# A two-layer hybrid decoder trunk on one core: inputs arranged in use order, and the triangular inverse with its small matmuls interleaved

## The chip, the cores and the metric

The kernel runs on one core of a Trainium2 chip. The metric is device time in microseconds (us) of one execution; the arrays are arranged on the host before the launch, and that is not part of the time. The time before is the median of three executions.

## What is computed

Two layers of the same form, on x of 256 positions by 2048 channels. One wide projection of the normalised input (7692 columns) feeds three mixers, whose gated outputs go together through one output projection and are added to x:

```python
for l in range(DEPTH):                      # DEPTH = 2, S = 256, D_MODEL = 2048
    h = rms_norm(x, norm_w[l])
    u = h @ w_in[l]                         # 2048 x 7692
    (c_in, c_gate, g_q, g_k, g_v, g_z, g_b, g_a, a_q, a_k, a_v, a_gate) = jnp.split(u, cuts, axis=-1)
    y_conv = conformer_conv(c_in, ...) * silu(c_gate)       # GLU, 31-tap depthwise conv, LayerNorm, 512 x 512
    y_gdn = gated_deltanet(g_q, g_k, g_v, g_z, g_b, g_a, ...)  # delta rule: a unit lower triangle is inverted
    y_att = dilated_attention(a_q, a_k, a_v, cos, sin) * silu(a_gate)
    x = x + jnp.concatenate([y_conv, y_gdn, y_att], axis=-1) @ w_out[l]
return rms_norm(x, final_norm_w)
```

## The kernel before

All work is written as tasks (Python generators) that name an engine, an estimated cost and the instruction. A planner, `Plan.run`, takes at each step the task that can start first by its estimates (then the lower priority number) and emits its instruction, so each engine's instruction stream is fixed when the program is built; on the chip each engine works through its stream in order and waits by semaphores.

TensorE (PE) carries the projections. A matrix product is made in three terms: weights and activations are each split in a rounded part and a remainder (`whi`, `wlo`; `HT[0]`, `HT[1]`), and hi*hi, hi*lo and lo*hi are added in PSUM. The two-row-block weight pieces (chunks: 256 rows by 384, 396 or 512 columns) are loaded by `load_weights` from the SP queue into four `RAW` buffers; ACT makes `whi` (line 182), DVE `wlo` (line 190), in three buffers each; `project` runs the chunks' matmuls (line 453) in a fixed list of jobs. The first job is GZ+384 (396 columns, 9 chunks in layer 0: two of one row block, then seven pairs), the second and third are the two K blocks of the delta rule, and so on; the convolution's pointwise product `conv_out` comes late in a layer, then two attention gates and the output projection in column pieces of 384, 384, 384, 384 and 512 (the last piece of layer 1 in two of 256). Two PSUM accumulators (`ACC`) alternate, so job 3 needs the accumulator of job 1 emptied; emptying it needs `rstd`, the row norms.

In layer 0, `load_x` brings x in six pieces by rows, in the same SP queue as the weights. PE transposes each 128 x 128 block (`norm_128`, line 230: 16 channel blocks by two row tiles), ACT and DVE scale by the norm weight and split into `HT`. `square_sums` (ACT) of the same buffers give the row norms, planned from 16 us on. `setup` loads the small parameters of a layer by rows (norm weights, short-conv weights, 31-tap weights, LayerNorm parameters, a_log, dt_bias), seven small DMAs and two broadcasts, and turns them by four PE transposes (line 339) and ACT copies into `MISC`, `CWT`, `DWT`.

`inverse` (layers 0 and 1) inverts twelve 128 x 128 unit triangles: 32 x 32 diagonal blocks on DVE, then the merge by small f32 matmuls on PE (all at line 223). In the first merge each head has matmuls of 32 x 32, in the second of 64 x 64. It is emitted in eight batches: for each of the two pairs of 32-row blocks (a, b) twelve matmuls into `psx[b]`, a DVE copy, twelve into `psy[a]` (and for the first pair twelve more into `psy[b]`); then for each half of the heads six into `psx`, a copy, six into `psy`. `psx` and `psy` are one PSUM tile each (128 partitions by 512 f32). Matmuls that follow each other inside a batch use the same rows and the same output partitions. The planner places projection matmuls between the batches.

## Time and profile before

| | us |
|---|---|
| median of three executions | 997.62 (996.41 to 998.58) |
| profiled execution, its own time | 998.17 |
| its span in the trace | 996.5 |
| PE busy | 983.1 (99%) |
| DVE busy | 749.7 (75%) |
| ACT busy | 551.9 (55%) |
| TensorE clock granted, mean | 0.997 |

The span is what the trace covers from the first instruction to the last; 1.67 us of the execution lie outside it. Busy time is the union of an engine's instructions; a matmul's record is longer than the distance to the next one, since matmuls are pipelined, so the distances between starts are what a stretch of PE costs. A record marked f32 by 32*32 is one pass; each f32 matmul makes two.

### The profile page before, as it was taken

How to read it: one execution, taken by the hardware profiler on the slowest of the kernel's cores; microseconds unless marked ns; L12 is line 12 of the kernel's file. 1: busy time of each engine (PE TensorE's matmuls, PEld its weight loads, DVE VectorE, ACT ScalarE, POOL GpSimd, SP SyncE). 2: the span in 40 equal slices, each digit the busy share in tenths (PEclk: the TensorE clock that was granted, in tenths of full speed). 3: DMA queues.
4: the chain of work that ended last, by engine and by line, in shares of the span. 5: the costliest groups of instructions: out<-in, count | busy, mean ns of one | idle time of the engine just before them, and what ended most of it. 6: DMA issues, size and time to landing. Idle time of an engine off the chain costs nothing.

```text
span 996.5 us, 19159 instructions
## 1 busy us (share of the span) xinstructions
PE 983.1 (99%) x7299; PEld 958.3 (96%) x7299; DVE 749.7 (75%) x1511; ACT 551.9 (55%) x1085; POOL 48.6 (5%) x70
## 2 busy tenths in 40 slices
PE   8999999999999999999999999999999999999996
PEld 7999999999999989999899999999999999999996
DVE  6587699988899666655557767999888987666672
ACT  7665345544676674454455633554447777545452
POOL 1000200200010000000000020002000101000000
PEclk9999999999999999999999999999999999999998
DMA  8665566644444635776766655666444456466772
GB/s 269 172 213 174 158 182 184 195 147 129 143 144 143 190 117 169 219 223 223 231 183 182 201 167 171 182 184 189 137 141 130 142 174 207 122 185 219 226 247 87
DMA packets 116585, 176.91 MB, mean 178 GB/s; under 512 B 8458, under 2 KB 97356, under 8 KB 116492
## 3 DMA queue, kind: packets, MB, share of 16 engines
q1 hardware_dynamic: 114572, 171.88, 56.4%
q0 software_dynamic: 1632, 3.02, 1.2%
q8 instruction: 57, 0.93, 0.4%
q10 hardware_dynamic: 288, 0.79, 0.2%
q14 instruction: 36, 0.29, 0.1%
HBM read 170.67 MB, written 4.98 MB: 176 GB/s over the span
## 4 chain that ended last, share of the span: by engine, by line
PE 97%; issue 1%; DMA 1%; DVE 0%; ACT 0%; SPq 0%; POOLq 0%; POOL 0%; DVEq 0%; ACTq 0%
PE acc L453 86%; PE mix L223 6%; PE mix L230 3%; DMA b<-in_x 1%; PE acc L462 1%; PE mix L751 0%; DVE wlo L190 0%; ACT b L182 0%; SPq L408 0%; DVE b L197 0%; SPq L390 0%; PE mix L339 0%; ACT whi L182 0%; POOLq L1300 0%; POOL rstd L239 0%
## 5 line engine op out<-in xcount | busy, mean ns | idle before, releaser
L182 ACT ACTIVATE whi<-raw 128x768 fp32r<-128x768 f32 (+4 forms) x389 | 339.7, 873 | 375.5 <-PE acc L453 319.0
L190 DVE TENSOR_TENSOR wlo<-raw,whi 128x768 fp32r<-128x768 f32 (+4 forms) x389 | 385.5, 991 | 193.0 <-ACT whi L182 186.2
L453 PE MATMUL acc<-HT,whi 128*128 128x256 f32 x2304 | 413.2, 281 | 0.0
L453 PEld LDWEIGHTS acc<-HT,whi 128*128 128x128 f32 x2304 | 352.0, 188 | 1.6 <-issue 1.5
L453 PE MATMUL acc<-HT,wlo 128*128 128x256 f32 x1152 | 321.7, 279 | 0.0
L453 PE MATMUL acc<-whi,HT 128*128 128x384 f32 (+1 forms) x1024 | 271.2, 346 | 0.0
L453 PEld LDWEIGHTS acc<-HT,wlo 128*128 128x128 f32 x1152 | 216.0, 188 | 0.0
L453 PEld LDWEIGHTS acc<-whi,HT 128*128 128x128 f32 x1024 | 179.8, 188 | 1.9 <-issue 1.0
L453 PE MATMUL acc<-wlo,HT 128*128 128x384 f32 (+1 forms) x512 | 172.6, 337 | 0.0
L453 PE MATMUL acc<-whi,YT 128*128 128x384 f32 (+2 forms) x640 | 162.8, 338 | 0.0
L453 PEld LDWEIGHTS acc<-whi,YT 128*128 128x128 f32 x640 | 114.2, 187 | 3.0 <-ACT whi L182 0.2
L453 PE MATMUL acc<-wlo,YT 128*128 128x384 f32 (+2 forms) x320 | 107.9, 337 | 0.4 <-DVE wlo L190 0.4
L187 DVE SCALAR_TENSOR_TENSOR b<-b,dw,b 128x255 f32<-128x255 f32 (+29 forms) x240 | 104.3, 461 | 0.2
L453 PEld LDWEIGHTS acc<-wlo,HT 128*128 128x128 f32 x512 | 96.1, 188 | 0.0
L453 PEld LDWEIGHTS acc<-wlo,YT 128*128 128x128 f32 x320 | 60.0, 187 | 2.2 <-DVE wlo L190 0.7
L230 PE MATMUL mix<-ident,b 128*128 128x128 f32 x312 | 51.2, 276 | 3.0 <-DMA b<-in_x 2.6
L182 ACT ACTIVATE b<-mix 128x256 f32<-128x256 f32 (+3 forms) x95 | 38.6, 422 | 19.1 <-PE mix L223 10.0
L187 DVE SCALAR_TENSOR_TENSOR b<-b,cw,b 128x255 f32<-128x255 f32 (+2 forms) x108 | 48.6, 473 | 0.0
L223 PE MATMUL mix<-b,b 128*128 128x128 f32 (+5 forms) x456 | 47.8, 285 | 0.4 <-ACT b L182 0.4
L230 PEld LDWEIGHTS mix<-ident,b 128*128 128x128 f32 x312 | 37.7, 140 | 8.3 <-DMA b<-in_x 3.5
L223 PEld LDWEIGHTS mix<-b,b 128*128 128x128 f32 (+3 forms) x456 | 38.0, 161 | 7.5 <-issue 2.7
L187 DVE SCALAR_TENSOR_TENSOR b<-b,b 128x256 f32<-128x256 f32 (+3 forms) x62 | 31.3, 510 | 2.7 <-ACT b L182 2.6
(149 smaller groups left out, 648.0 us busy)
## 6 DMA issues: line engine op xcount, KB each, us to landing
raw<-in_w_in SPq DMA_DIRECT2D x240, 384.0 KB, 3.1
raw<-in_w_in SPq DMA_DIRECT2D x48, 512.0 KB, 3.5
raw<-in_w_out SPq DMA_DIRECT2D x64, 384.0 KB, 3.8
raw<-in_w_out SPq DMA_DIRECT2D x12, 512.0 KB, 5.4
raw<-in_w_in SPq DMA_DIRECT2D x15, 396.0 KB, 4.6
raw<-in_conf_pw_w SPq DMA_DIRECT2D x4, 512.0 KB, 3.7
raw<-in_w_out SPq DMA_DIRECT2D x8, 256.0 KB, 4.2
b<-in_x SPq DMA_DIRECT2D x6, 256.0 KB
```

Of the source, the lines that this page charges most:

```text
L182: lambda: nc.scalar.activation(out_, in_, func, bias=bias, scale=scale, **kw))
L187: lambda: nc.vector.scalar_tensor_tensor(out_, a, s, b, op0=op0, op1=op1))
L190: return ("dve", 70 + _free(out_) / 0.96, lambda: nc.vector.tensor_tensor(out_, a, b, op=op))
L223: nc.tensor.matmul(o, a, b, start=f[0], stop=f[1])
L230: nc.tensor.transpose(o, a, ident)
L453: nc.tensor.matmul(o, w, m, start=first and i == 0 and not (chan and t % 2), stop=last and i == 2, skip_group_check=chan)
L462: nc.tensor.matmul(acc[t][:, :n], YT[w][:, k, s], HT[m][:, k, :n], start=k == 0 and i == 0, stop=k == KB - 1 and i == 2)
```

## The change

x is given twice: as before (`x`), and by channel (`x_t`: 128 partitions by 16 channel blocks by 256 positions). `load_xt` and `norm_xt` load `x_t` ahead of the first nine weight chunks and split it straight from SBUF into `HT`; the 32 PE transposes of layer 0's input are gone. x by rows is loaded in eight pieces of 256 columns ahead of weight chunks 8 to 15 and serves only the square sums. The parameters of a layer come as one array (128 by 237) by one DMA, for layer 0 on the ACT queue; the PE transposes of `setup` are gone, two scalings by 0.5 move to DVE. The weights are laid out on the host column block by column block and in pairs of row blocks, so that a chunk has one contiguous run per partition (3072 bytes for a 384 column pair, 1536 twice before). In `inverse` the two pairs of 32-row blocks share one first batch and one second batch, matmul by matmul in turn; the second of the four 64-wide batches and the third are joined in the same way: five batches for eight. Its matmuls are the same ones. The planner's costs are unchanged, but its order follows from the tasks, so the streams are laid anew.

```diff
-    CWT = [cp.tile([128, 72], F32, name=f"cw{l}") for l in range(DEPTH)]
-    DWT = [cp.tile([128, 124], F32, name=f"dw{l}") for l in range(DEPTH)]
-    MISC = [cp.tile([128, 30], F32, name=f"misc{l}") for l in range(DEPTH)]
-    AD = [cp.tile([128, 2, H], F32, name=f"ad{l}") for l in range(DEPTH)]
+    PAR = [cp.tile([128, PCOLS], F32, name=f"par{l}") for l in range(DEPTH)]
+    GNH = [cp.tile([128, 1], F32, name=f"gnh{l}") for l in range(DEPTH)]
     AEXP = [cp.tile([128, H], F32, name=f"aexp{l}") for l in range(DEPTH)]
-    PIECES = [(384 * i, 384) for i in range(4)] + [(1536, 512)]
-    LAST_PIECES = PIECES[:4] + [(1536, 256), (1792, 256)]
+    PIECES, LAST_PIECES = W_OUT_BLOCKS
     GROUPS = [(0, 768), (768, 768), (1536, 512)]
-    X_PIECES = [(256 * i, 256) for i in range(4)] + [(1024, 512), (1536, 512)]
-    X_BEFORE = {0: 0, 2: 1, 3: 2, 4: 3, 5: 4, 7: 5}
+    X_PIECES = [(256 * i, 256) for i in range(8)]
+    XT_BEFORE = {0: (0, 1), 1: (1, 1), **{i: (2 * i - 2, 2) for i in range(2, 9)}}
+    X_BEFORE = {8 + j: j for j in range(len(X_PIECES))}
     SSQ = [cp.tile([128, NT, len(p)], F32, name=f"ssq{l}")
            for l, p in enumerate([X_PIECES] + [PIECES] * (DEPTH - 1) + [LAST_PIECES])]
...
 
-        def turn(dst, srcs, scale=1.0, cost=100.0):
-            st = yield ("get", S256)
-            r = sum(n for _, n in srcs)
-
-            def emit():
-                o = 0
-                for src, n in srcs:
-                    nc.sync.dma_start(st[o:o + n, :128], src)
-                    o += n
-            yield ("dma", cost * len(srcs), emit)
-            ps = yield ("get", MIX)
-            yield ("pe", 107.0, lambda: nc.tensor.transpose(ps[:, :r], st[:r, :128], ident[:r, :r]))
-            yield act(dst, ps[:, :r], scale=scale)
-            yield ("put", MIX, [ps])
-            yield ("put", S256, [st])
-
-        def col(p):
-            return p[l].rearrange("(c p) -> c p", p=128)
         if l:
             yield ("wait", conv_ready[0])
-        yield from turn(MISC[l][:, 0:16], [(col(norm_w), 16)], cost=0.0 if l == 0 else 100.0)
+        yield ("dma", 200.0 if l else 0.0, lambda: (nc.sync if l else nc.scalar).dma_start(PAR[l], params[l]))
         yield ("set", misc_ready[l])
-        for e in x_loaded if l == 0 else []:
-            yield ("wait", e)
-        yield from turn(CWT[l], [(conv_qkv_w[l].rearrange("j (c p) -> (j c) p", p=128), 72)])
-
-        def emit():
-            for i, p in enumerate((a_log, dt_bias)):
-                nc.sync.dma_start(AD[l][:, i], bass.AP(tensor=p.tensor, offset=p.offset + l * H,
-                                                       ap=[[0, 128], [1, H]]))
-        yield ("dma", 200.0, emit)
-        yield act(AEXP[l], AD[l][:, 0], AF.Exp)
-        yield from turn(DWT[l], [(conf_dw_w[l].rearrange("j (c p) -> (j c) p", p=128), 124)], 0.5)
-        yield from turn(MISC[l][:, 16:29], [(col(conf_dw_b), 4), (col(conf_ln_w), 4), (col(conf_ln_b), 4),
-                                            (gdn_norm_w[l:l + 1], 1)])
-        yield ts(MISC[l][:, 29:30], MISC[l][:, 28:29], 0.5, None, ALU.mult)
+        yield act(AEXP[l], PAR[l][:, P_AL:P_AL + H], AF.Exp)
+        yield ts(PAR[l][:, P_DW:P_DW + 4 * CW], PAR[l][:, P_DW:P_DW + 4 * CW], 0.5, None, ALU.mult)
+        yield ts(GNH[l], PAR[l][:, P_GN:P_GN + 1], 0.5, None, ALU.mult)
         yield ("set", conv_ready[l])
 
...
+        base += rows * c0
         for k, m in order:
-            chunks.append((w[k * 128:(k + m) * 128, c0:c0 + n], m, n, k if keep else None))
+            src = bass.AP(tensor=wt.tensor, offset=wt.offset + base + (k // 2) * 256 * n + (k % 2) * n,
+                          ap=[[2 * n, 128]] + ([[256 * n, m // 2]] if m > 2 else []) + [[1, min(m, 2) * n]])
+            chunks.append((src, m, n, k if keep else None))
             for lst in (raw_ready, w_ready):
                 lst.append([Event(), None])
         return first
 
+    def load_xt(k0, m):
+
+        buf = yield ("get", S768)
+        yield ("dma", 128 * m * S * 4 / 330.0, lambda: nc.sync.dma_start(
+            buf[:, :m * S], bass.AP(tensor=x_t.tensor, offset=x_t.offset + k0 * S, ap=[[KB * S, 128], [1, m * S]])))
+        plan.spawn(norm_xt(k0, m, buf), 2)
+
+    def norm_xt(k0, m, buf):
+        yield ("wait", misc_ready[0])
+        for b in range(m):
+            k = k0 + b
+            yield from split(HT[0][:, k, :], HT[1][:, k, :], buf[:, b * S:(b + 1) * S], PAR[0][:, k:k + 1])
+            yield ("set", h_ready[0][k])
+        yield ("put", S768, [buf])
+
     def load_x(j):
 
         c0, n = X_PIECES[j]
-        pool = S768 if n < 512 else S1024
-        buf = yield ("get", pool)
+        buf = yield ("get", S768)
         xs = buf[:, :NT * n].rearrange("p (t c) -> p t c", t=NT)
         yield ("dma", 128 * NT * n * 4 / 330.0, lambda: nc.sync.dma_start(
             xs, xf[:, c0:c0 + n].rearrange("(t p) c -> p t c", p=128)))
-        plan.spawn(norm_block(0, j, (c0, n), [xs[:, t] for t in range(NT)], nsq0[j], pool, [buf], SUMS_FROM), 2)
-        if j == 0:
-            plan.spawn(setup(0), -2).base = 0.0
+        plan.spawn(sums_x(j, xs, buf), 3)
         if j == len(X_PIECES) - 1:
             nc.sync.dma_start(lncs, lnc)
             nc.sync.dma_start(ropes, rope.rearrange("(t p) c -> p t c", p=128))
-        yield ("set", x_loaded[j])
+
+    def sums_x(j, xs, buf):
+        yield from square_sums(0, j, [xs[:, t] for t in range(NT)], nsq0[j])
+        yield ("put", S768, [buf])
 
     def load_weights(order):
         for i in order:
             src, m, n, _ = chunks[i]
+            if i in XT_BEFORE:
+                yield from load_xt(*XT_BEFORE[i])
             if i in X_BEFORE:
                 yield from load_x(X_BEFORE[i])
             raw = yield ("get", RAW)
             view = raw[:, :m * n].rearrange("p (a n) -> p a n", n=n)
+            flat_ = raw[:, :m * n]
+            if m > 2:
+                flat_ = flat_.rearrange("p (a n) -> p a n", n=2 * n)
             raw_ready[i][1] = (raw, view)
-            yield ("dma", 128 * m * n * 4 / 330.0, lambda src=src, view=view: nc.sync.dma_start(
-                view, src.rearrange("(a p) n -> p a n", p=128)))
+            yield ("dma", 128 * m * n * 4 / 330.0,
+                   lambda src=src, flat_=flat_: nc.sync.dma_start(flat_, src))
             yield ("set", raw_ready[i][0])
 
...
-            for p, (a, b) in enumerate(prs):
-                yield mms(*((psx[b, hc * 32:hc * 32 + 32], Lh(hc)[a, b], T3[a, hc, :]) for hc in range(HC)))
+            yield mms(*((psx[b, hc * 32:hc * 32 + 32], Lh(hc)[a, b], T3[a, hc, :]) for hc in range(HC) for a, b in prs))
+            for a, b in prs:
                 yield cpy(Xs[b, :, :32], h3(psx[b, :HC * 32], 32))
-                yield mms(*((psy[a, hc * 32:hc * 32 + 32], Xs[b, hc, :32], P3[b, hc, :]) for hc in range(HC)))
-                if p == 0:
-                    yield mms(*((psy[b, hc * 32:hc * 32 + 32], P3[b, hc, :], Xs[b, hc, :32]) for hc in range(HC)))
-                    yield ts(T64[b, :, a], h3(psy[b, :HC * 32], 32), -1.0, None, ALU.mult)
+            (a0, b0), (a1, b1_) = prs
+
+            def third(hc):
+                c = slice(hc * 32, hc * 32 + 32)
+                return [(psy[a0, c], Xs[b0, hc, :32], P3[b0, hc, :]), (psy[a1, c], Xs[b1_, hc, :32], P3[b1_, hc, :]),
+                        (psy[b0, c], P3[b0, hc, :], Xs[b0, hc, :32])]
+            yield mms(*(m for hc in range(HC) for m in third(hc)))
+            yield ts(T64[b0, :, a0], h3(psy[b0, :HC * 32], 32), -1.0, None, ALU.mult)
+            for a, b in prs:
                 yield ts(PTs[a, :, b], h3(psy[a, :HC * 32], 32), -1.0, None, ALU.mult)
             yield ("put", S384, [Pd, Td])
             a, b = slice(0, 64), slice(64, 128)
-            for i in range(2):
-                hs = slice(i * H, (i + 1) * H)
-                yield mms(*((psx[b, j * 64:j * 64 + 64], Lh(i * H + j)[a, b], T64[:, i * H + j, :])
-                            for j in range(H)))
-                yield cpy(Xs[b, hs, :], h3(psx[b, :H * 64], 64))
-                yield mms(*((psy[a, j * 64:j * 64 + 64], Xs[b, i * H + j, :], PTs[b, i * H + j, b])
-                            for j in range(H)))
-                yield ts(PTs[a, hs, b], h3(psy[a, :H * 64], 64), -1.0, None, ALU.mult)
+
+            def down(i, j):
+                return (psx[b, j * 64:j * 64 + 64], Lh(i * H + j)[a, b], T64[:, i * H + j, :])
+
+            def up(i, j):
+                return (psy[a, j * 64:j * 64 + 64], Xs[b, i * H + j, :], PTs[b, i * H + j, b])
+            hs = [slice(i * H, (i + 1) * H) for i in range(2)]
+            yield mms(*(down(0, j) for j in range(H)))
+            yield cpy(Xs[b, hs[0], :], h3(psx[b, :H * 64], 64))
+            yield mms(*(m for j in range(H) for m in (down(1, j), up(0, j))))
+            yield cpy(Xs[b, hs[1], :], h3(psx[b, :H * 64], 64))
+            yield ts(PTs[a, hs[0], b], h3(psy[a, :H * 64], 64), -1.0, None, ALU.mult)
+            yield mms(*(up(1, j) for j in range(H)))
+            yield ts(PTs[a, hs[1], b], h3(psy[a, :H * 64], 64), -1.0, None, ALU.mult)
             yield ("put", MIX, [psx, psy])
             yield ("put", INV, [b1])
...
     plan.spawn(warm_up(5), 0, 5000.0)
-    for l in range(1, DEPTH):
-        plan.spawn(setup(l), 40)
+    for l in range(DEPTH):
+        plan.spawn(setup(l), 40 if l else -2)
     plan.spawn(finish_norm(0, nsq0), 3)
     all_jobs = []
     for l in range(DEPTH):
...
 
 
-_INS = ["x", "norm_w", "w_in", "conv_qkv_w", "a_log", "dt_bias", "gdn_norm_w", "conf_dw_w", "conf_dw_b",
-        "conf_ln_w", "conf_ln_b", "conf_pw_w", "w_out", "final_norm_w"]
+def _blocks(w, blocks):
+
+    return np.concatenate([w[:, c0:c0 + n].reshape(-1, 2, 128, n).transpose(0, 2, 1, 3).ravel() for c0, n in blocks])
+
+
+def _layouts(x, norm_w, w_in, conv_qkv_w, a_log, dt_bias, gdn_norm_w, conf_dw_w, conf_dw_b, conf_ln_w, conf_ln_b,
+             conf_pw_w, w_out, final_norm_w):
+    def col(p):
+        return p.reshape(-1, 128).T
+
+    def every(p):
+        return np.broadcast_to(p, (128, p.size))
+    params = np.stack([np.concatenate([col(norm_w[l]), col(conv_qkv_w[l]), col(conf_dw_w[l]), col(conf_dw_b[l]),
+                                       col(conf_ln_w[l]), col(conf_ln_b[l]), col(gdn_norm_w[l]), every(a_log[l]),
+                                       every(dt_bias[l])], axis=1) for l in range(DEPTH)])
+    assert params.shape == (DEPTH, 128, PCOLS)
+    return {"x": x, "x_t": x[0].reshape(S, KB, 128).transpose(2, 1, 0),
+            "w_in": np.concatenate([_blocks(w, W_IN_BLOCKS) for w in w_in]),
+            "conf_pw_w": np.concatenate([_blocks(w, [(0, 512)]) for w in conf_pw_w]),
+            "w_out": np.concatenate([_blocks(w, b) for w, b in zip(w_out, W_OUT_BLOCKS)]),
+            "params": params, "final_norm_w": final_norm_w}
 
 
```

## Rows read from the trace of the kernel before

**Rows 1.** The page: busy time by engine, and the chain that ended last.
```profile
PE 983.1 (99%) x7299; PEld 958.3 (96%) x7299; DVE 749.7 (75%) x1511; ACT 551.9 (55%) x1085; POOL 48.6 (5%) x70
...
PE 97%; issue 1%; DMA 1%; DVE 0%; ACT 0%; SPq 0%; POOLq 0%; POOL 0%; DVEq 0%; ACTq 0%
```

**Rows 2.** Windows at the start: length, busy PE PEld DVE ACT POOL, clock, DMA share, GB/s.
```profile
0.00:5.00 5.00, 3.41 (x16) 3.05 (x17) 2.04 (x1) 1.63 (x3) 3.43 (x12) 1.00 0.51 149
5.00:10.00 5.00, 2.38 (x16) 1.81 (x14) 2.92 (x6) 3.35 (x7) 0.00 (x0) 1.00 0.92 294
10.00:15.00 5.00, 4.98 (x32) 4.64 (x33) 3.99 (x7) 3.29 (x7) 0.00 (x0) 1.00 1.04 375
```

**Rows 3.** Timeline of PE, job 1: start, us, instruction [idle before <-releaser].
```profile
7.32 0.66 PE L230 MATMUL mix<-ident,b 128*128 128x128 f32 x4 [1.68 <-DMA b<-in_x]
7.74 0.61 PE L453 MATMUL acc<-whi,HT 128*128 128x396 f32 x2
...
10.02 0.66 PE L230 MATMUL mix<-ident,b 128*128 128x128 f32 x4 [0.95 <-DMA b<-in_x]
...
14.40 1.04 PE L230 MATMUL mix<-ident,b 128*128 128x128 f32 x8
...
21.61 0.61 PE L453 MATMUL acc<-whi,HT 128*128 128x396 f32 x2
...
29.28 0.27 PE L339 MATMUL mix<-ident,b 124*128 124x124 f32 x1
```

**Rows 4.** Timelines of ACT and of DVE, the first weight chunks.
```profile
4.84 0.53 ACT L182 ACTIVATE whi<-raw 128x396 fp32r<-128x396 f32 x1 [0.42 <-DMA raw<-in_w_in]
...
9.23 0.86 ACT L182 ACTIVATE whi<-raw 128x792 fp32r<-128x792 f32 x1 [0.38 <-DMA raw<-in_w_in]
...
5.41 0.57 DVE L190 TENSOR_TENSOR wlo<-raw,whi 128x396 fp32r<-128x396 f32 x1 [1.19 <-ACT whi L182]
...
10.13 0.98 DVE L190 TENSOR_TENSOR wlo<-raw,whi 128x792 fp32r<-128x792 f32 x1 [0.36 <-ACT whi L182]
```

**Rows 5.** Timeline of PE around the inverse of layer 0.
```profile
212.82 0.84 PE L223 MATMUL mix<-b,inv 32*32 32x32 f32 x21
213.48 0.21 PE L223 MATMUL mix<-inv,b 32*32 32x32 f32 x1
213.51 0.19 PE L223 MATMUL mix<-b,inv 32*32 32x32 f32 x1
...
214.35 0.44 PE L230 MATMUL mix<-ident,b 128*128 128x128 f32 x2
...
217.64 0.34 PE L453 MATMUL acc<-wlo,HT 128*128 128x384 f32 x1
217.90 0.94 PE L223 MATMUL mix<-b,b 32*32 32x32 f32 x24
218.77 0.62 PE L453 MATMUL acc<-whi,HT 128*128 128x384 f32 x2
...
219.41 0.52 PE L453 MATMUL acc<-whi,HT 128*128 128x384 f32 x2
...
224.28 0.91 PE L223 MATMUL mix<-T,b 64*64 64x64 f32 x12
```

**Rows 6.** Timeline of PE: full f32 matmuls; two 64-row halves in turn.
```profile
194.35 0.83 PE L223 MATMUL mix<-b,b 128*128 128x128 f32 x6
...
341.45 1.58 PE L223 MATMUL mix<-b,b 64*128 64x128 f32 x16
```

**Rows 7.** Windows, late in the projection of layer 0.
```profile
300.00:310.00 10.00, 10.00 (x63) 9.87 (x62) 9.65 (x28) 8.19 (x20) 0.00 (x0) 1.00 0.47 143
```

**Rows 8.** Timeline of PE just before `conv_out` of layer 0.
```profile
367.36 0.70 PE L230 MATMUL mix<-ident,b 128*128 128x128 f32 x3 [0.36 <-DVE b L197]
368.50 1.24 PE L223 MATMUL mix<-b,b 128*64 128x256 f32 x8 [0.44 <-ACT b L182]
```

**Rows 9.** Windows at the end, PE idle.
```profile
990.00:995.00 5.00, 0.00 (x0) 0.00 (x0) 1.16 (x3) 0.94 (x1) 0.55 (x1) 0.63 0.56 211
```

35 lines of the change are left out of this document (19 added, 16 removed).

## The prediction

> **What bounds the kernel now.** I read the page first, then the windows at the start, then PE's own timeline there, then PE around the inverse. The page says that PE is busy for 99% of the span and that 97% of the chain which ended last is PE [rows 1]. DVE has 75%, ACT 55%. So time is won only by work that leaves PE's stream, or by PE's waits. The waits lie at the start: in the first 10 us PE is busy for 5.79 us, while the DMA share climbs to 0.92 and then to 1.04 at 375 GB/s [rows 2]. From 10.4 us PE never stops in job 1. Outside the start there are short waits just before `conv_out` of layer 0 [rows 8]. The tail after the last matmul is not touched.
>
> **The start of job 1.** Today the weights of row block 0 are ready at 5.41 + 0.57 = 5.98 us [rows 4], but their matmuls start at 7.74: four transposes of the next piece of x stand before them in PE's stream and wait 1.68 us for that piece; two pieces later the same costs 0.95 us [rows 3]. Between the matmuls lie further transposes, eight in a row at 14.40. Job 1 ends at 29.28.
>
> With `x_t` nothing of x passes through PE. Bytes ahead of block 0's weights in the queues: `x_t` 131 KB, the weights 203 KB and the 121 KB of parameters (on ACT's queue, but the same DMA engines), 455 KB against 473 KB before (x 262, norm weights 8, weights 203). So the weights land at about the same 4.84, and block 0 starts at about 6.0. Then the loads set the pace. The first pair of row blocks is ready when `wlo` of chunk 2 is done: today 10.13 + 0.98 = 11.11 [rows 4]. The bytes ahead of it are the same except the parameters, which give 121 KB / 350 GB/s = 0.35 us (rate between the windows' 294 and 375 [rows 2]). So 11.45 us. A row block costs (29.28 - 21.61) / 7 = 1.096 us [rows 3], seven blocks less 0.03 for a transpose among them, and 14 blocks 15.3 us: job 1 ends at 26.8, a gain of **2.5 us**. The later chunks keep up by a little: ACT's 0.86 and DVE's 0.98 for a chunk [rows 4] and the splits of two `HT` blocks fit in the 2.19 us that PE takes for a pair. Bounds: if PE waited for nothing after 6.0, the end would be 23.5, a gain of 5.8; if the loads fall behind further, 0. I take 2.5, since the chunk that decides is one whose landing a row shows.
>
> Waits that are added: every `HT` split waits for the parameters' DMA, and behind the first of them in ACT's stream stands `whi` of chunk 0; ACT has 0.42 us of idle ahead of that now [rows 4]. A landing a microsecond later than I think would move block 0 and 1, not chunk 2, which decides. The gap that PE has between row blocks 1 and 2 grows to some 2.7 us. The granted clock fell after PE had stood idle at the end, to a mean of 0.63 in that window [rows 9]; should it fall to 1.2 GHz here, matmuls double for a while and it could eat the whole 2.5.
>
> **x by rows, read again.** It adds 2.1 MB on the SP queue ahead of chunks 8 to 15 and moves the two table loads behind it. A piece and a chunk are 262 + 393 KB per 2.1 us, 312 GB/s at worst, under the 375 of a full window [rows 2], and weight buffers run ahead by several chunks. The square sums end later than now, near 32 us, and with them the row norms. Nobody on PE asks for them before job 3 needs job 1's accumulator, at about 26.8 + 17 = 44 us. Cost 0; beyond 12 us of delay each further one would be paid in full. The bytes of the weights are the same, their runs are longer, and PE waits for none of them outside the start: 0.
>
> **Small parameters.** Six PE transposes of `setup` fall behind the end of job 1 (the others are in the sum above). One record lasts 0.27 us [rows 3]; in a stream it pushes the next matmul by at least its columns and at most that and a change of operands. Bounds 0.03 and 0.27 each, so 0.2 to 1.6; nearest is a transpose in a row of eight, 1.04 / 8 = 0.13, and I take 0.15: **0.9 us**. Two new DVE scalings of small tiles run where DVE is idle.
>
> **The inverse.** A pass of a 32 x 32 matmul costs (214.35 - 212.82) / 48 = 0.032 us. A batch costs more: from 217.64 to 218.77 are 1.13 us, less one 384 column pass (7.67 / 42 x 384 / 396 = 0.177, from job 1's blocks [rows 3]) is 0.953; the pair behind it takes 0.62 instead of 0.52. So 1.05, of which 24 passes are 0.77 and the borders 0.28. A 64 x 64 pass: 0.91 for 12, less 0.17 of the last one's tail (0.94 - 0.77 in the 24), is 0.06 [rows 5]. Per layer now: 120 x 0.032 + 48 x 0.06 + 7 places x 0.28 = 8.7 us.
>
> Do passes on different parts of the array overlap? When the batch into `psy[a]` gives way to that into `psy[b]`, the new batch's first pass starts at 213.48 and the old one's next at 213.51, in turn and without a drain [rows 5]: same rows, different output partitions, one PSUM tile. In attention, halves of 64 rows alternate, into two PSUM tiles: eight passes of 128 and eight of 256 columns last 1.58 us together. A full pass of 128 columns costs about 0.83 / 6 = 0.14 at most, or 0.11 without the tail, so one after the other these would take 8 x 0.11 + 8 x 0.22 = 2.6 us [rows 6]. They overlap.
>
> After, with overlap: batch one 48 passes in the time of 24, 0.77; batch two has three streams, and since only a few passes were seen to run ahead, I take it between two and three abreast, 0.95; then 0.72 each for the three 64-wide batches; five borders 1.4. Together 5.28, a gain of 3.4 a layer, **6.8 us** in all. Bounds: all three abreast 7.2; no overlap at all, 120 x 0.032 + 48 x 0.06 + 1.4 = 8.1, a gain of 1.1 from three borders less a layer.
>
> The DVE copies and negations are as many as before; they now wait for longer batches, and PE fills that time with projection work, as it does now.
>
> **Sum.** 2.5 + 0.9 + 6.8 = 10.2 us. The profiled execution took 998.17 (span 996.5 and 1.67 around it), which gives 988.0; it lay 0.55 above the median, so 987.4 against 997.62.
>
> **The rivals.**
>
> *Overlap only across PSUM tiles.* No row shows two row groups writing one PSUM tile at once, and batch one and the second stream of batch two do just that. If these are taken one after the other, batches one and two cost 1.54 each, a layer 6.6, the gain is 2.1 a layer and the time 990.0. For it: nothing in the trace; against it: the `psy` passes overlap in one tile, though from the same rows. The Trainium skill, "TensorEngine Tiling (Array Packing)", section "Restrictions and Gotchas", states that different row tiles cannot access the same PSUM bank simultaneously; by that rule the sum would be this rival's, and no run here shows it yet.
>
> *The gain of layer 0 is waited away.* In layer 0 DVE is busy for 9.65 of 10 us late in the projection [rows 7], and PE already waits 0.36 us for DVE and 0.44 us for ACT ahead of `conv_out` [rows 8]. If the depthwise convolution on DVE ends no earlier, PE reaches `conv_out` 3.4 us sooner and waits there: 990.8. Against it: windows before that have DVE idle, and the chain behind the convolution is placed late by the planner, not by need.
>
> *It does not overlap.* The alternation brings nothing, only fewer borders: 2.5 + 0.9 + 1.1 = 4.5, so 993.1. Against it rows 5 and 6.
>
> *Slower: a drain at each change of place.* The borders of a batch cost 0.28 us, 0.14 a side. If PE paid such a border at each change from one part of the array to another inside the new batches (24 + 36 + 12 changes a layer, 144 in all), this would add 144 x 0.14 = 20.2 us to a gain of 4.5: 1013. It turns the sign from 0.03 us a change on. Against it: alternating passes at 213.48 show none [rows 5].
>
> **How the numbers follow.** Forecast 987.4, chance 0.55 (its own range 984 to 989). Overlap across tiles only 0.20. Layer 0 waited away 0.12. No overlap 0.08. Drain 0.05. The range from 983.5 (start at the better half of its bounds, three abreast) to 992.5 holds the first three. A measurement here tells apart about 0.2%, 2 us: faster 0.91, same 0.04 (no overlap, and the start's gain lost to the clock or the loads), slower 0.05.
>
> **What would show it.** The end of job 1 near 26.8 and its first matmul near 6.0; no record of lines 230 and 339 before the row norms; five batches a layer at line 223, the first lasting about 0.94 us and not 1.7; the wait ahead of `conv_out` not longer than now. Wrong would be: PE idle at `conv_out` for over 2 us, a clock of 0.5 after the gap near 9 us, or a first batch that costs 48 passes.

## The result, and the profile after

The changed kernel takes 984.42 us (median of four executions, 982.40 to 984.86), the kernel before 997.98 beside it (996.41 to 998.58): a ratio of 0.9863, 95% interval 0.9845 to 0.9881. The forecast was 987.4, its range 983.5 to 992.5. The sign and the bound came out as written, and the gain is a third larger: 13.6 us for 10.2. Over all nine executions of the changed kernel in this study the median is 983.01 (981.88 to 984.86), half a microsecond below the low end of the range: nearly every piece of the gain came out larger than forecast.

The page of the changed kernel, busy time, chain, and DMA packets, beside [rows 1]:

```profile
PE 968.4 (99%) x7259; PEld 946.3 (96%) x7259; DVE 749.3 (76%) x1519; ACT 550.8 (56%) x1079; POOL 48.5 (5%) x70
...
DMA packets 67037, 179.01 MB, mean 183 GB/s; under 512 B 8000, under 2 KB 12224, under 8 KB 66944
...
PE 97%; DVE 1%; DMA 1%; issue 1%; SPq 0%; ACT 0%; POOLq 0%; POOL 0%; DVEq 0%; ACTq 0%
```

PE is the bound as before; it is busy for 14.7 us less, and 40 instructions are gone from it (the 32 transposes of x and the eight of `setup`). DVE and ACT do what they did. So the whole gain is PE's stream getting shorter, as the forecast had it. Where it got shorter is read from the stretches between two projection matmuls of the same number (there are 6144 in both kernels, in the same order):

| stretch (us) | before | after, first trace | after, second trace |
|---|---|---|---|
| start of the span to the end of job 1 (no. 96) | 29.31 | 25.45 | 25.50 |
| no. 96 to 1000 (parameters' transposes lie here) | 113.86 | 110.88 | 112.50 |
| no. 1400 to 2000 (inverse of layer 0) | 137.04 | 132.98 | 132.93 |
| no. 2000 to 2400 (`conv_out` of layer 0) | 58.05 | 56.72 | 56.72 |
| no. 4400 to 5000 (inverse of layer 1) | 138.64 | 135.50 | 135.48 |
| last projection matmul starts | 988.28 | 972.10 | 973.97 |

The first trace is of the execution of 982.40, the second of one of 984.27 (e5 below). They differ by 1.6 us in one stretch and by little elsewhere; that is a matter of the matmuls' pace and stands in the last section. Without it the gains are 3.8, 1.4, 4.1, 1.3 and 3.2 us, 13.8 together, and half a microsecond in small pieces. Behind the last projection matmul 0.4 us of this is lost again: the span ends 8.6 us after that matmul's start for 8.2 before, with the same instructions. Why was not followed.

The start. Windows (length, busy PE PEld DVE ACT POOL, clock, DMA share, GB/s), which answer [rows 2]; x is read again from 13.5 to 27 us:

```profile
0.00:5.00 5.00, 3.42 (x16) 3.40 (x17) 2.82 (x5) 2.31 (x4) 3.43 (x12) 1.00 0.58 157
5.00:10.00 5.00, 3.90 (x16) 2.50 (x15) 3.14 (x6) 3.12 (x6) 0.00 (x0) 1.00 0.97 325
...
20.00:25.00 5.00, 5.00 (x30) 5.00 (x29) 2.86 (x5) 4.86 (x15) 0.00 (x0) 1.00 1.05 380
25.00:30.00 5.00, 5.00 (x43) 5.00 (x42) 2.58 (x3) 4.49 (x15) 0.00 (x0) 1.00 1.01 342
```

Timeline of PE in job 1 (start, us, instruction, in brackets the idle time before it and who ended it), which answers [rows 3], then ACT's and DVE's for chunks 0, 2 and 3, which answer [rows 4]:

```profile
4.70 1.01 PE L448 MATMUL acc<-whi,HT 128*128 128x396 f32 x2
...
8.79 0.63 PE L448 MATMUL acc<-whi,HT 128*128 128x396 f32 x2 [0.58 <-ACT whi L188]
9.81 0.45 PE L448 MATMUL acc<-wlo,HT 128*128 128x396 f32 x1 [0.39 <-DVE wlo L196]
...
12.70 0.45 PE L448 MATMUL acc<-wlo,HT 128*128 128x396 f32 x1 [0.39 <-DVE wlo L196]
...
25.45 0.40 PE L448 MATMUL acc<-HT,whi 128*128 128x256 f32 x2
```

```profile
4.09 0.52 ACT L188 ACTIVATE whi<-raw 128x396 fp32r<-128x396 f32 x1
...
7.87 0.86 ACT L188 ACTIVATE whi<-raw 128x792 fp32r<-128x792 f32 x1 [0.20 <-DMA raw<-in_w_in]
...
10.76 0.86 ACT L188 ACTIVATE whi<-raw 128x792 fp32r<-128x792 f32 x1 [0.56 <-DVE HT L193]
...
8.77 0.98 DVE L196 TENSOR_TENSOR wlo<-raw,whi 128x792 fp32r<-128x792 f32 x1 [0.57 <-ACT whi L188]
```

Block 0 starts 3 us earlier than before. Then PE waits three times for weights to be ready, 1.36 us together, and from 12.70 on never again in job 1. The last wait is not for the same chunk in every trace. In the two others of the changed kernel, e5's and then e11's, PE's last wait in job 1 is for `wlo` of chunk 2:

```profile
10.59 0.45 PE L448 MATMUL acc<-wlo,HT 128*128 128x396 f32 x1 [0.39 <-DVE wlo L196]
...
10.03 0.45 PE L448 MATMUL acc<-wlo,HT 128*128 128x396 f32 x1 [0.39 <-DVE wlo L196]
```

In the two later windows above, where x is read again, the DMA share is 1.05 and 1.01, and PE is busy for the whole 5.00.

The inverse of layer 0, PE's timeline, which answers [rows 5]:

```profile
202.83 0.95 PE L229 MATMUL mix<-b,b 32*32 32x32 f32 x48
203.71 0.61 PE L448 MATMUL acc<-whi,HT 128*128 128x384 f32 x2
...
207.02 0.22 PE L229 MATMUL mix<-b,inv 32*32 32x32 f32 x2
207.04 0.21 PE L229 MATMUL mix<-inv,b 32*32 32x32 f32 x1
...
207.91 0.44 PE L236 MATMUL mix<-ident,b 128*128 128x128 f32 x2
```

The 48 passes of batch one take 203.71 - 202.83 = 0.88 us to the next projection matmul; before, 24 passes took 218.77 - 217.90 = 0.87 [rows 5]. The 72 passes of batch two, three streams, take 207.91 - 207.02 = 0.89. So two streams and three streams both cost what one costs. The three begin within 0.02 us of each other. The fourth batch, two 64-wide streams joined, takes 0.845 us to the next matmul, and a single 64-wide stream 0.838.

Two more places. Ahead of `conv_out` PE goes from one projection matmul to the next, without the two waits of [rows 8]; in layer 1's inverse there are two new ones:

```profile
355.79 0.28 PE L448 MATMUL acc<-HT,wlo 128*128 128x256 f32 x1
355.90 0.40 PE L448 MATMUL acc<-YT,whi 128*128 128x256 f32 x2
...
699.78 0.27 PE L229 MATMUL mix<-T,b 64*64 64x64 f32 x1 [0.29 <-DVE inv L209]
...
703.63 0.91 PE L229 MATMUL mix<-PTs,inv 64*64 64x64 f32 x12 [0.58 <-DVE PTs L203]
```

### The profile page after: what moved, and what is told of

It reads as the page before. It is cut to its first block, busy times and chain, and to the rows that moved or that the text cites. A ratio compares the mean times of both kernels' runs of the same rounds, so it can differ in the third digit from the quotient of the medians.

```text
span 980.7 us, 19060 instructions
## 1 busy us (share of the span) xinstructions
PE 968.4 (99%) x7259; PEld 946.3 (96%) x7259; DVE 749.3 (76%) x1519; ACT 550.8 (56%) x1079; POOL 48.5 (5%) x70
## 4 chain that ended last, share of the span: by engine, by line
PE 97%; DVE 1%; DMA 1%; issue 1%; SPq 0%; ACT 0%; POOLq 0%; POOL 0%; DVEq 0%; ACTq 0%
PE acc L448 87%; PE mix L229 6%; PE mix L236 3%; DMA b<-in_x_t 1%; PE acc L457 1%; PE mix L747 0%; DVE wlo L196 0%; DVE b L193 0%; SPq L404 0%; SPq L362 0%; DVE inv L209 0%; ACT whi L188 0%; POOLq L1327 0%; POOL rstd L245 0%; DVE PTs L203 0%
## 5 line engine op out<-in xcount | busy, mean ns | idle before, releaser
L193 DVE SCALAR_TENSOR_TENSOR b<-b,par,b 128x255 f32<-128x255 f32 (+20 forms) x348 | 153.6, 465 | 0.3
L188 ACT ACTIVATE b<-mix 128x384 f32<-128x384 f32 (+3 forms) x96 | 39.6, 425 | 20.1 <-PE mix L229 12.6
L236 PE MATMUL mix<-ident,b 128*128 128x128 f32 x280 | 45.7, 274 | 0.0
L236 PEld LDWEIGHTS mix<-ident,b 128*128 128x128 f32 x280 | 34.2, 140 | 3.7 <-issue 1.3
L188 ACT ACTIVATE b<-b,stat 128x128 f32<-128x128 f32 (+1 forms) x68 | 29.1, 442 | 6.0 <-DVE stat L203 5.9
```

Of the source, the lines that this page charges most:

```text
L188: lambda: nc.scalar.activation(out_, in_, func, bias=bias, scale=scale, **kw))
L193: lambda: nc.vector.scalar_tensor_tensor(out_, a, s, b, op0=op0, op1=op1))
L236: nc.tensor.transpose(o, a, ident)
```

## Experiments

Theory: the gain is the sum of three separate pieces, x by channel, the parameters' transposes, and the overlap of the inverse's small matmuls. Rivals: the inverse gains from fewer batches and not from overlap; the long runs of the weights or the earlier DMA issue give the start's gain; the second reading of x has a price that does not show.

The table gives the same stretches for each kernel; times are medians, the kernel before being measured beside each group (998.21 for e1 to e4, 997.35 for e5 to e8, 998.27 for e9 to e11, 998.34 for e12).

| kernel | time | to no. 96 | 96 to 1000 | 1400 to 2000 | 2000 to 2400 | 4400 to 5000 |
|---|---|---|---|---|---|---|
| e1 inverse only | 989.67 | 29.05 | 113.84 | 132.98 | 56.73 | 135.41 |
| e2 layouts only | 991.25 | 25.21 | 110.87 | 137.04 | 58.05 | 138.63 |
| e3 merged, in order | 986.35 | 25.52 | 110.87 | 135.51 | 56.72 | 136.92 |
| e4 weights by rows | 983.11 | 25.74 | 110.87 | 132.98 | 56.72 | 135.48 |
| e6 parameters by rows | 984.78 | 25.46 | 113.95 | 132.93 | 56.72 | 135.41 |
| e7 x by rows | 987.02 | 28.45 | 112.52 | 132.98 | 56.73 | 135.40 |
| e8 sums late | 996.12 | 27.13 | 122.81 | 132.92 | 56.73 | 135.41 |
| e9 finer start, later copies | 989.00 | 27.12 | 112.48 | 132.38 | 61.25 | 134.40 |
| e10, the same kernel again | 985.77 | 25.09 | 112.48 | 132.38 | 60.05 | 134.39 |
| e12 later copies in layer 1 | 981.25 | 25.17 | 110.88 | 132.98 | 56.73 | 134.40 |

**e1_inverse_only: the kernel before with the new inverse.**

```diff
-            for p, (a, b) in enumerate(prs):
-                yield mms(*((psx[b, hc * 32:hc * 32 + 32], Lh(hc)[a, b], T3[a, hc, :]) for hc in range(HC)))
...
+            yield mms(*((psx[b, hc * 32:hc * 32 + 32], Lh(hc)[a, b], T3[a, hc, :]) for hc in range(HC) for a, b in prs))
...
```

> The kernel before with the interleaved inverse alone. If the terms add, it gains what PE's stream shows in the changed kernel's inverse, 3.5 us a layer: 991.0 us, with the first merge batch of 48 passes lasting about 0.95 us. Rival: layer 0's share is waited away ahead of conv_out, where PE of the kernel before already waits some 1.8 us: then only layer 1 gains and it is 994.5 us, with a longer wait near 365 us.

989.67 (988.76 to 990.23), ratio 0.9915, interval 0.9902 to 0.9929: a gain of 8.5 us, of which 4.06 and 3.23 lie in the two inverses and 1.32 in the stretch of `conv_out`. The rest moved by 0.3 us or less a stretch, 0.8 us together.

**e2_layouts_only: the changed kernel with the old inverse.**

```diff
-            yield mms(*((psx[b, hc * 32:hc * 32 + 32], Lh(hc)[a, b], T3[a, hc, :]) for hc in range(HC) for a, b in prs))
...
+            for p, (a, b) in enumerate(prs):
+                yield mms(*((psx[b, hc * 32:hc * 32 + 32], Lh(hc)[a, b], T3[a, hc, :]) for hc in range(HC)))
...
```

> The changed kernel with the inverse of before. If the terms add: 984.4 + 7.0 = 991.4 us. Rival: the wait ahead of conv_out is gone because of the inverse and not because of the layouts; then it comes back here and the time is about 993 us.

991.25 (990.64 to 993.63), ratio 0.9935, interval 0.9923 to 0.9948: 7.0 us. The two halves of the change sum to 8.5 + 7.0 = 15.5, somewhat more than the whole's 13.6, and close to the 15 us by which the median of all nine executions lies below the kernel before; the trace of e2 has the quicker pace in the stretch 96 to 1000 (1.6 us), which some executions of the whole lack. With the old inverse the waits ahead of `conv_out` are back:

```profile
360.26 0.70 PE L236 MATMUL mix<-ident,b 128*128 128x128 f32 x3 [0.37 <-DVE b L203]
361.40 1.25 PE L229 MATMUL mix<-b,b 128*64 128x256 f32 x8 [0.43 <-ACT b L188]
```

So those waits go and come with the inverse. That they go with the planner's new order of work, and not with the time that the overlap saves, shows in e3, which has no overlap and not these waits either (56.72).

**e3_merged_in_order: the changed kernel, the same five batches, but inside a batch one stream after the other.**

```diff
-            ... for hc in range(HC) for a, b in prs))
+            ... for a, b in prs for hc in range(HC)))
...
-            yield mms(*(m for hc in range(HC) for m in third(hc)))
+            yield mms(*(third(hc)[i] for i in range(3) for hc in range(HC)))
...
-            yield mms(*(m for j in range(H) for m in (down(1, j), up(0, j))))
+            yield mms(*[down(1, j) for j in range(H)], *[up(0, j) for j in range(H)])
```

> The changed kernel with its five batches, but inside the three joined batches one stream follows the other instead of taking turns. If the alternation makes the overlap: batch one +0.77 us, batch two +1.3, batch four +0.7, so 2.8 us a layer: 990.0 us. Rival: the fewer borders are the gain and the order inside a batch is indifferent: 984.4 us.

986.35 (986.01 to 986.43), ratio 0.9882, interval 0.9869 to 0.9896. PE's timeline in layer 0:

```profile
202.89 1.60 PE L229 MATMUL mix<-b,b 32*32 32x32 f32 x48
204.42 0.61 PE L448 MATMUL acc<-whi,HT 128*128 128x384 f32 x2
...
207.73 1.50 PE L229 MATMUL mix<-b,inv 32*32 32x32 f32 x45
...
209.92 0.44 PE L236 MATMUL mix<-ident,b 128*128 128x128 f32 x2
```

Batch one now takes 1.53 us to the next projection matmul and not 0.88, batch two 2.19 and not 0.89: order alone makes the difference, with the same number of batches and of passes. Batch four takes 1.36 and not 0.845. Layer 0 loses 2.53 us by it. Layer 1 loses only 1.42, because its two waits for DVE (1.1 us, e12 below) are not there when the batches are slower. The two together are the 4.0 us between this trace's execution (986.40) and the first trace's (982.40), which have the same pace. The time falls between the two expectations because of layer 1, and because both started from 984.4, 2 us above the execution of that trace. The rival has a part in it: five batches in order still take 1.5 us less in layer 0 than the kernel before (135.51 for 137.04), and 1.7 in layer 1. So of layer 0's 4.1 us the alternation is worth 2.5, the five batches and the order that came with them 1.5.

**e4_weights_by_rows: the changed kernel with the weights in memory as before.**

```diff
-            src = bass.AP(tensor=wt.tensor, offset=wt.offset + base + (k // 2) * 256 * n + (k % 2) * n, ...)
+            src = w[k * 128:(k + m) * 128, c0:c0 + n]
```

> The changed kernel with the weights in HBM as before (two runs of 1536 or 1584 bytes per partition and chunk instead of one of 3072 or 3168). If the long runs brought chunk 2 in at 7.85 us instead of 9.2 us, it lands late again here and job 1 ends near 26.8 us: 985.7 us. Rival: the earlier issue and the fewer bytes ahead did it, the runs nothing: job 1 ends near 25.5 us and the time is 984.4 us.

983.11 (982.58 to 983.53), against 983.01 for the changed kernel: the longer runs bring nothing that the time shows. Job 1 ends 0.2 to 0.8 us later than in the three traces of the changed kernel, which differ by 0.6 among themselves, so a few tenths at the start remain possible.

**e5_after_again: the changed kernel itself, no edit.**

> The changed kernel once more, beside the other kernels of this call. Time: 984.4. Its trace answers a question that the earlier traces raised: the 256 column projection matmuls follow each other at 113.3 ns in some stretches and at 117.8 ns in the others; in the changed kernel the fast stretch is 95.0 to 136.3 us. If the pace belongs to the program (same instructions, same moments), the same stretch is fast again; if each execution falls into one of the two at random, another stretch is.

982.58 (982.11 to 984.27), ratio 0.9852, interval 0.9837 to 0.9866. Its trace is the "second trace" of the first table: the stretch that was quick in the first trace ran at 117.8 ns here. The pace is not a property of the program alone.

**e6_parameters_by_rows: the changed kernel with `setup` as before; only layer 0's norm weights stay on the ACT queue.**

```diff
-        yield ("dma", 200.0 if l else 0.0, lambda: (nc.sync if l else nc.scalar).dma_start(PAR[l], params[l]))
+        yield from turn(par[:, P_CW:P_CW + 72], [(conv_qkv_w[l].rearrange("j (c p) -> (j c) p", p=128), 72)])
+        ...
+        yield from turn(par[:, P_DB:P_DB + 13], [...])
```

> The changed kernel with the small parameters brought as before: by rows, with small DMAs, PE transposes and ACT copies; only layer 0's norm weights stay on the ACT queue in their new layout, so that the start is not touched. My theory: the six transposes cost what they cost in the trace of the kernel before (0.03 + 0.25 + 0.25 + 0.03 + 0.03 + 0.27 beyond the matmuls' own pace), so 984.4 + 0.9 = 985.3. Rival: the parameters' part is the whole 2.98 us that the stretch behind job 1 became shorter, 987.4. Rival: nothing, 984.4. Between them stands the pace of the matmuls (113 or 118 ns) from 95 to 136 us: if that follows the parameters' transposes, 1.6 us more than my figure, 986.9, and the trace shows it.

984.78 (984.36 to 985.25). The stretch 96 to 1000 is 113.95, 1.45 longer than in e5's trace at the same pace of the matmuls. So the parameters' transposes are worth 1.4 us, and the other 1.6 of the 2.98 in the first trace are the pace. Single records show that the six are of two kinds. One of 13 rows:

```profile
35.00 0.28 PE L484 MATMUL acc<-HT,wlo 128*128 128x256 f32 x1
35.20 0.23 PE L340 MATMUL mix<-ident,b 13*128 13x13 f32 x1
35.36 0.50 PE L484 MATMUL acc<-HT,whi 128*128 128x256 f32 x2
35.70 0.28 PE L484 MATMUL acc<-HT,wlo 128*128 128x256 f32 x1
```

From the matmul ahead of it to the third one behind are 0.70 us for three distances of 0.118: it costs 0.35 us. The matmul just behind comes 0.25 late, and the one after that another 0.1 (0.22 for 0.118). With 72 or 124 rows the first distance is 0.15 and the second 0.20, so such a transpose costs 0.12. Three of each kind make 1.4 us, which is what the stretch shows. The expectation had looked at the first distance alone; that the median lies near its 985.3 all the same is chance, since it started from 984.4.

**e7_x_by_rows: the changed kernel with x brought by rows and transposed on PE.**

```diff
-    XT_BEFORE = {0: (0, 1), 1: (1, 1), **{i: (2 * i - 2, 2) for i in range(2, 9)}}
-    X_BEFORE = {8 + j: j for j in range(len(X_PIECES))}
+    X_BEFORE = {0: 0, 2: 1, 3: 2, 4: 3, 5: 4, 7: 5}
```

> The changed kernel with x brought as before: six pieces by rows ahead of the first weight chunks, 32 PE transposes, no copy by channel and no second reading. My theory, from the two traces: the start gave 3.9 us, so 984.4 + 3.9 = 988.3, job 1 ending near 29.3. Rival: the start's part is the 2.5 of the forecast and the rest came with the parameters (their DMA on another queue, issued 0.5 us earlier), 986.9, job 1 ending near 28. If the 113 ns pace from 95 to 136 us is lost too, 1.6 more in either case.

987.02 (986.61 to 987.79), 4.0 us above the changed kernel. PE's timeline:

```profile
6.86 1.11 PE L236 MATMUL mix<-ident,b 128*128 128x128 f32 x4 [0.23 <-DMA b<-in_x]
7.62 0.97 PE L428 MATMUL acc<-whi,HT 128*128 128x396 f32 x2
...
28.45 0.40 PE L428 MATMUL acc<-HT,whi 128*128 128x256 f32 x2
```

Block 0 waits again behind the transposes of the second piece of x. Job 1 ends 2.95 us later than in e5's trace, and 0.86 earlier than in the kernel before. So x by channel is worth 3.0 us of the start's 3.8. The other 0.8 belong to what e7 kept: the parameters' way (no norm weights on the SP queue and no transposes of theirs on PE) and the weights' longer runs, for which e4 leaves a few tenths open. These are not separated. The time is the rival's, since it sits beside a median to which both paces contribute; the trace lies between the two expectations.

**e8_sums_late: the changed kernel, the second reading of x eight chunks later.**

```diff
-    X_BEFORE = {8 + j: j for j in range(len(X_PIECES))}
+    X_BEFORE = {16 + j: j for j in range(len(X_PIECES))}
```

> The changed kernel with the second reading of x moved 8 weight chunks back (ahead of chunks 16 to 23), so that the square sums end some 8 x 2.12 = 17 us later, near 51. It tests the price of nothing for that reading and the margin that the forecast gave it. By the forecast's margin of 12 us: 5 us of waiting ahead of job 3, 989.4. By the trace of the changed kernel (sums done at 33.7, job 3 from 42.4, some 3 us of chain between): a margin of 5.7, so 11 us of waiting, 995.7. Rival: nobody on PE waits for the sums at all, 984.4.

996.12, a single execution. PE's timeline ahead of job 3; then a window there (busy PE PEld DVE ACT POOL, clock, DMA share, GB/s); then POOL in this run and in the changed kernel, and in the latter PE's first matmuls of job 3:

```profile
51.62 0.69 PE L236 MATMUL mix<-ident,rstd 128*128 128x128 f32 x2 [7.37 <-POOL rstd L245]
53.25 0.80 PE L448 MATMUL acc<-HT,whi 128*128 128x256 f32 x2 [0.94 <-ACT b L188]
...
50.00:56.00 6.00, 3.43 (x15) 3.04 (x16) 4.02 (x16) 2.94 (x10) 0.71 (x1) 0.50 0.01 4
...
50.86 0.71 POOL L245 TENSOR_TENSOR rstd<-rstd,pw_neg 128x2 f32<-128x2 f32 x1 [46.73 <-DVE rstd L205]
...
34.24 0.71 POOL L245 TENSOR_TENSOR rstd<-rstd,pw_neg 128x2 f32<-128x2 f32 x1 [30.11 <-DVE rstd L205]
...
42.63 0.40 PE L448 MATMUL acc<-HT,whi 128*128 128x256 f32 x2
```

POOL takes up `rstd` 16.6 us later than in the changed kernel. PE was 1.7 later itself before the wait, so job 3 would have started at 42.6 + 1.7 = 44.3; it starts at 53.25, 8.95 later. The margin in the changed kernel is therefore 16.6 - 1.7 - 8.95 = 6.0 us, not the forecast's 12. The stretch 96 to 1000 is 10.3 longer, more than that wait, because the granted clock fell during it: to its lower level, 0.50 from 50 to 56 us. The twenty matmuls from 53.25 on take 3.74 us, where they take 2.36 in the changed kernel, and the other 1.4 us are that. So waiting cost more than the wait. The time lies near the expectation's 995.7 partly by chance: 11 us of waiting were expected, and 9 came, with 1.4 of the clock here and 1.6 of the clock in job 1 (last section).

**e9_finer_start: four single row blocks at the start, and the planner told that three of the inverse's DVE operations cost 0.7 us more.**

```diff
-    XT_BEFORE = {0: (0, 1), 1: (1, 1), **{i: (2 * i - 2, 2) for i in range(2, 9)}}
+    XT_BEFORE = {**{i: (i, 1) for i in range(4)}, **{i: (2 * i - 4, 2) for i in range(4, 10)}}
-        halved = [(0, 1), (1, 1)] + full[1:]
+        halved = [(i, 1) for i in range(4)] + full[2:]
...
-            yield cpy(Xs[b, hs[0], :], h3(psx[b, :H * 64], 64))
+            yield late(cpy(Xs[b, hs[0], :], h3(psx[b, :H * 64], 64)))
```

> The changed kernel with two edits against the waits that its traces still show: in layer 0 the first four row blocks of job 1 come as single ones (weights and x by channel), and the planner is told that three of the inverse's 64-wide DVE operations cost 0.7 us more than it thinks, so that it lays more projection work ahead of the batches that wait for them. My theory: the two waits in layer 1's inverse (1.2 us together) go, and of the 1.4 to 2.0 us that PE waits in job 1 between row blocks about half goes: 983.6 (median of the eight executions of the changed kernel so far) - 1.2 - 0.8 = 981.6. Rival: DVE is as busy around layer 1's inverse as before and the waits only move, and the finer pieces cost ACT and DVE as much as PE gains: 983.6. Rival: more and smaller pieces on the queue delay the later chunks, 985.

989.00 (988.17 to 989.45), ratio 0.9906, interval 0.9891 to 0.9921: 6 us slower than the changed kernel, a miss of all three expectations. Layer 1's waits went (134.40 for 135.50) and layer 0's inverse gained 0.6 too, but PE now waits for DVE ahead of `conv_out` of layer 0. The trace of e10, the same kernel:

```profile
359.14 1.16 PE L240 MATMUL mix<-ident,b 128*128 128x128 f32 x6 [2.17 <-DVE b L203]
```

The stretch 2000 to 2400 is 60.05 there and 61.25 in e9, for 56.72. The further 1.2 in e9 come from the granted clock, which fell behind this wait too (0.68 in the window from 360 to 365 us, 1.00 in e10). Whether the later copies in layer 0 or the finer start brought the wait is not separated: e12 below leaves out both. The finer start did not help either: in e9's trace job 1 ends at 27.12, because the granted clock fell in it (last section), in e10's at 25.09.

**e10_after_third: the kernel of e9 once more.**

> The kernel of the run before this one, once more on the same chip, for its trace: the pace of the 256 column projection matmuls behind the eighteen f32 matmuls near 92 us. If the pace (113.3 or 117.8 ns) is drawn anew in each execution, two traces of one kernel on one chip can differ there; if it belongs to the chip or the program, they agree.

985.77, with a granted clock of 1.00 in every window of job 1. The mean granted clock is 0.998 in this execution and 0.994 to 0.996 in the five of e9, and the 3.2 us between 985.77 and the 989.00 of e9's trace are the 2.0 of job 1 and the 1.2 behind the wait. Both traces of this kernel, on one chip, have 117.8 ns in the stretch in question, so they agree.

**e11_after_fourth: the changed kernel once more, beside e9 and e10.**

> The changed kernel itself once more, on the same chip as the two runs before, for the same question: so far the stretch from 95 to 136 us ran at 113.3 ns in one trace of it and at 117.8 ns in the other, which were taken on different chips. Time 982 with the faster pace, 984 with the slower.

981.88, with the 113.3 ns pace from 94.5 to 135.8 us, as in its first trace and unlike e5's.

**e12_later_copies_layer_1: the changed kernel, the planner's 0.7 us in layer 1 alone.**

```diff
+            def late(op):
+                return (op[0], op[1] + 700.0 * l, op[2])
...
-            yield cpy(Xs[b, hs[0], :], h3(psx[b, :H * 64], 64))
+            yield late(cpy(Xs[b, hs[0], :], h3(psx[b, :H * 64], 64)))
```

> The changed kernel with one edit: the planner is told 0.7 us more for three of the inverse's 64-wide DVE operations, in layer 1 alone; layer 0 and the start stay as they are. My theory: layer 1's two waits for DVE (0.29 and 0.58 us of idle, 1.1 us in the stretch) go, as in the run with both edits, and nothing else moves, because layer 0's wait ahead of conv_out came from the same edit in layer 0: 983.0 (median of nine executions of the changed kernel) - 1.1 = 981.9. Rival: the wait ahead of conv_out comes from the finer start, or layer 1 now pays one ahead of its own conv_out: 983.0 or more.

981.25 (980.98 to 983.41), ratio 0.9836, interval 0.9823 to 0.9849. PE's timeline in layer 1's inverse, where two waits stood:

```profile
700.18 0.27 PE L229 MATMUL mix<-T,b 64*64 64x64 f32 x1
...
705.38 0.91 PE L229 MATMUL mix<-PTs,inv 64*64 64x64 f32 x12
```

No wait is left, the stretch is 1.10 shorter, and `conv_out` of layer 0 is untouched. Against the changed kernel the executions overlap (981.88 to 984.86); that it is quicker rests on the trace.

## Why the prediction was right, step by step

**The bound, and the sum from PE's stream: right.** Nearly all of the gain is five stretches of PE's stream, and the pieces add up: 3.8 + 1.4 + 4.1 + 3.2 + 1.3. Of these the last was forecast as nothing and the first four at 2.5, 0.9, 3.4 and 3.4. The errors do not cancel: all but layer 1's are on the same side, and the range held because it was wide.

**The start: right mechanism, mis-sized, 3.8 for 2.5.** Two times were off. Block 0 started at 4.70 and not near 6.0: ACT takes up its weights at 4.09 for 4.84 [rows 4], since 131 KB of `x_t` stand ahead of them where 262 KB of x and the norm weights stood, and its first two matmuls need only `whi`, ready at 4.61, while the forecast waited for `wlo`. This did not set the end. The end is set by PE's last wait. In e5's and e11's traces that is the wait for chunk 2, which the forecast had named, but at 10.59 and 10.03 and not 11.45; job 1 ends 14.9 us later in both (25.50 and 24.93), where the forecast had 15.3. In the first trace chunk 2 was ready sooner still, at 8.77 + 0.98 = 9.75, and the last wait is for chunk 3, at 12.70, 12.75 us ahead of the end. So the step that was mis-sized is "11.45": chunk 2 was ready 0.9 to 1.7 us sooner. The likely reason is the rate of the queues, 325 to 342 GB/s from 5 to 10 us in the three traces, where [rows 2] has 294. Which edit raised it is not separated: it is 316 with the old weight runs (e4) and 346 with the old x (e7).

**The small parameters: right mechanism, mis-sized, 1.4 for 0.9.** The forecast took 0.15 us each from a transpose in a row of eight. Between projection matmuls three of the six cost 0.12 and three 0.35, beyond the forecast's upper bound of 0.27 (e6): not only the next matmul comes late but the one after it too.

**The inverse: right mechanism, just past the upper bound.** 4.1 and 3.2 us for 3.4 a layer, 7.3 where the bound was 7.2. Three streams run abreast, not "between two and three": batch two takes as long as batch one, so its passes cost 0.77 in the forecast's reckoning and not 0.95. The sum also counts seven places in the kernel before where there are eight batches; with eight it is 3.7 a layer, and 3.9 with three abreast. What layer 0 gained beyond that came with the planner's new order and was not followed. Layer 1's 3.2 is what is left after 1.1 us of new waits for DVE; without them (e12) it is 4.2. The alternation is worth 2.5 us a layer where nothing waits (e3).

**What the forecast had as nothing.** x read again: nothing, as written, but on a margin of 6.0 us and not 12 (e8). POOL took up the row norms 2.2 us after the forecast's end of the sums (34.2 for 32), job 3 came 1.4 sooner (42.6 for 44), and the forecast left out that from there to job 3 are 2.4 us (53.25 - 50.86 in e8), in which POOL makes the norms, PE turns them and ACT empties the accumulator. Longer runs: nothing (e4). The wait ahead of `conv_out`: the forecast let it stay, and it went, 1.3 us, together with the new inverse (e1 and e3 have it, e2 has not).

**The rivals.** *Overlap only across PSUM tiles* is refuted for this kernel: batch one writes one PSUM tile from two row groups into two ranges of output partitions, 48 passes in 0.88 us alternating and 1.53 in order. The Trainium skill, "TensorEngine Tiling (Array Packing)", section "Restrictions and Gotchas", states that different row tiles cannot access the same PSUM bank simultaneously. The price that the rival drew from it does not agree with the trace, 0.88 us for 1.53. Whether two of the writes ever fall in the same instant no trace shows: they go to different output partitions, and 48 passes of 32 columns at the pace of the long matmuls (113.3 ns / 256 x 32 = 14 ns, an estimate) are 0.68 us, so they could also take turns. In batch two 72 of them would be 1.02 us and took 0.89, so there some passes do run at the same time; which ones is open. *No overlap* falls by the same rows, though fewer batches in order brought 1.5 us of layer 0's gain (e3) where this rival had 0.6. *A drain at each change* falls too: 48 passes that change place each time take as long as 24 that do not. *Layer 0's gain waited away* did not happen, but e9 and e10 show how near it was: with other edits PE waits 2.17 us for DVE at this place, and the stretch is 60 us for 56.7.

## What to carry to other kernels

In this kernel small matmuls on different parts of the array run abreast if they follow each other in turn, even into one PSUM tile with different output partitions; in order they do not. When loads set the pace of a start, look for the last chunk that PE waits for, not the first: waits for earlier ones are absorbed. Look at more than one trace for it, since the chunk can change. The price of a small instruction in PE's stream is read over the two matmuls behind it and not over one. An order that a planner lays out by estimates has waits for a busy engine at places where the estimates are low; telling it more helped there (e12), and with two further edits it cost more than it gave (e9).

## What the runs showed of the hardware that was not expected

**Two paces of the same matmuls at the same granted clock.** Windows of the projection line alone (busy PE and PEld, clock, DMA share, GB/s), first trace of the changed kernel, then e5's:

```profile
110.00:120.00 10.00, 10.00 (x90) 10.00 (x90) 1.00 0.52 170
120.00:130.00 10.00, 10.00 (x91) 10.00 (x90) 1.00 0.62 206
```

```profile
110.00:120.00 10.00, 10.00 (x88) 10.00 (x87) 1.00 0.57 161
120.00:130.00 10.00, 10.00 (x88) 10.00 (x87) 1.00 0.65 194
```

The same 365 matmuls of 256 columns in a row follow each other at 113.3 ns in the one and at 117.8 in the other, 1.6 us in the stretch. In the stretches looked at the pace changes only where other matmuls interrupt the stream, and holds at least until the next interruption. What sets it is open: the changed kernel had the quicker one in two of its three traces, e2, e3, e4 and e12 had it, and the kernel before, e1 and e6 to e10 had not, in this stretch. Neither the program nor the chip alone decides it: e9 and e10 on the one hand, e11 and e12 on the other ran on the same chip. A comparison of two profiles of this kernel carries 1.6 us of it; the first trace of the changed kernel, at 982.40 the fastest of its four executions, flattered the change by that.

**The granted clock in job 1.** In e9's trace it fell after PE had waited 1.33 us near 11 us: from 13.95 to 16.92 the matmuls of 396 columns follow each other at 0.33 us and not at 0.18. Windows of e9, then of e5, where a wait of 1.33 us brought no fall:

```profile
10.00:15.00 5.00, 3.27 (x14) 2.62 (x13) 3.44 (x7) 3.73 (x7) 0.00 (x0) 0.87 1.03 389
15.00:20.00 5.00, 5.00 (x24) 5.00 (x23) 4.22 (x8) 4.03 (x9) 0.00 (x0) 0.79 1.04 355
```

```profile
10.00:15.00 5.00, 4.61 (x26) 4.41 (x25) 4.34 (x9) 4.45 (x9) 0.00 (x0) 1.00 1.03 386
```

e8's trace has the same fall (0.67 in the window from 10 to 15 us). Job 1 ends at 27.12 in e9 for 25.09 in e10, and at 27.13 in e8 for 25.50 in e5: some 1.6 to 2 us, the danger that the forecast had named for a gap at this place. It struck none of the three traces of the changed kernel. The windows do not tell all of it: in e12 the matmuls of job 1 also follow each other at 0.33 us from 5.5 to 7.2, where the windows show 1.00, and job 1 ended no later for that (25.17).

**A transpose of 13 or 16 rows between projection matmuls costs 0.35 us, one of 72 or 124 rows 0.12** (e6). The first is near the border that the inverse's batches of 32 rows pay, 0.28 in the forecast's reckoning. That both are the change to a smaller part of the array is a guess, and was not tried by itself.
